# Gated delta stage: triangles of all heads ahead of the state chains, x and half the head tiles through HBM, substitution on 128 partitions, output projection in two halves

## The chip, the cores and the metric

The kernel runs on one core of a Trainium2 chip. The metric is the time of one execution on the device in microseconds; the median of several executions is given, and one execution has been taken with the hardware profiler. Engines: PE (matmuls), DVE, ACT and POOL (elementwise work), SP (issues the DMA transfers). Matmuls write PSUM, everything else is in SBUF, 128 partitions.

## What is computed

A mixer block, an MLP, then a second block with a gated delta rule layer, a feed-forward layer (ffn0), windowed attention, another feed-forward layer and a last norm; 512 positions, width 1024. The change touches the gated delta layer only:

```python
def gated_delta_rule_chunked(q, k, v, beta, g):          # 8 heads of 128, chunks
    gc = jnp.cumsum(g, axis=-1)
    diff = gc[..., :, None] - gc[..., None, :]
    decay = jnp.exp(jnp.where(incl, diff, -jnp.inf))
    kb = k * beta[..., None]
    Lmat = jnp.where(strict, jnp.einsum('bhnid,bhnjd->bhnij', kb, k) * decay, 0.0)
    rhs = jnp.concatenate([v * beta[..., None], kb * jnp.exp(gc)[..., None]], axis=-1)
    sol = lax.linalg.triangular_solve(eye + Lmat, rhs, left_side=True, lower=True, unit_diagonal=True)
    attn_intra = jnp.einsum('bhnid,bhnjd->bhnij', q, k) * decay
    ...
    def step(state, xs):
        v_new = val - jnp.einsum('bhcd,bhde->bhce', kcd, state)
        o = jnp.einsum('bhcd,bhde->bhce', qd, state) + jnp.einsum('bhij,bhje->bhie', a_c, v_new)
        state = state * gl[..., None, None] + jnp.einsum('bhcd,bhce->bhde', kd, v_new)

def deltanet_mixer(h, w_in, conv_w, A_log, dt_bias, onorm_g, w_out):
    p = h @ w_in                        # 8 heads x (k, q, v, gate), and 16 columns for b, a
    qkv = jax.nn.silu(causal_dwconv(qkv, conv_w))        # then l2norm of q and k
    o = gated_delta_rule_chunked(q, k, v, beta, g)
    o = rmsnorm_2(o, onorm_g) * jax.nn.silu(gate)
    return o.reshape(Bsz, S, A_V) @ w_out                # added to x
```

## The kernel before

Activations lie transposed, features on partitions: x is eight tiles `x0` to `x7` of 128 x 512 fp32. A linear layer makes one output tile of 128 x 512 by eight contraction steps of three matmuls of 512 columns each (`mm3`, L266 to L268): both operands are split into a high and a low part, and high by high, low by high and high by low are added in PSUM. Such an output tile, 24 matmuls, is called a unit here. Its weights come by one DMA of 512 KB (L241, on SP's queue); ACT makes the high part (L242) and DVE the low part (L243). Three buffers for weights are in use in turn.

The in projection of the delta layer has 32 such units: k, q, v for each of eight heads (`projected`, after which `conv4` makes the short convolution and its activation), and eight gates (`delta_gate`). Five units (`AHEAD`) are computed in `delta_begin`, then the per-position scalars (`delta_scalars`), and the other 27 are a generator `fill` that serves as filler.

A head goes through four steps. `delta_a` transposes k, q and v by blocks of 128 (L632 is the helper's transposes, L618 that of the outputs), takes squares for the norms, an inverse square root on POOL, builds the decay tile (`decay`), the triangle `LT` and the tile `AT` by small matmuls, writes the diagonal 32 x 32 blocks of `LT` to HBM (L755, four DMAs per head), and scales k and v on ACT (L758, L759) into `kd` and `vb`. `delta_solve(g)` takes the blocks of four heads back, one 32 x 32 triangle per partition on 64 partitions (L773), and inverts them by substitution in 30 steps of two DVE instructions (L780 the outer product, L782 the addition), then sends the result through HBM into the transposed layout (L785, L787). `delta_merge(g)` makes the inverses of 128 x 128 from those of 32 x 32 in small matmuls with copies between (L818, L830, L836, L845, L852). `delta_c(h)` runs the chain over four blocks: state, values, outputs (L868 to L879), each step waiting for a DVE or ACT instruction; at its end come the norm of the output (scaling at L903) and the transposition back. `gated(h)` multiplies by the gate and splits high and low (L300, L301). The output projection (`OutProj` with `a_w_out`, eight units over all heads) adds each unit to x (L967).

`weave` takes generators, each with a count of steps, and interleaves their instructions in proportion to these counts in program order, which is then the order on each engine. The order before: 4 units with `delta_a` of heads 0 and 1; 3 with head 2; 3 with head 3; 6 with the first substitution; 1 with the first merge; 1 with the chains 0 to 3; 3 with heads 4 to 7's triangles; 5 with the second substitution; `gated` 0 to 3; 1 with the second merge; the last ones and four contraction steps of the output projection's first three tiles with the chains 4 to 7; `gated` 4 to 7; the rest of the output projection. SBUF tiles of 128 x 512 come from a pool of 44 (`hid`).

## Time and profile before

| | us |
|---|---|
| median of three executions | 1948.19 (1948.05 to 1948.5) |
| the profiled execution | 1945.63 |
| its span, first to last instruction | 1943.8 |
| PE busy in the span | 1860.1 (96%) |
| DVE busy | 1227.8 (63%) |
| ACT busy | 825.9 (42%) |
| mean granted clock of PE | 0.972 of full speed |

The profile has a page with the busy time of each engine, the span in 40 slices, the DMA queues, the chain of work that ended last, the groups of instructions by line, and the DMA issues. The trace behind it can be asked for stretches, for groups by line and form, for waits and for instructions in order of time. Busy time of PE says that a matmul is under way, not that it runs at full clock: the granted clock stands beside it.

### The profile page before, as it was taken

How to read it: one execution, taken by the hardware profiler on the slowest of the kernel's cores; microseconds unless marked ns; L12 is line 12 of the kernel's file. 1: busy time of each engine (PE TensorE's matmuls, PEld its weight loads, DVE VectorE, ACT ScalarE, POOL GpSimd, SP SyncE). 2: the span in 40 equal slices, each digit the busy share in tenths (PEclk: the TensorE clock that was granted, in tenths of full speed). 3: DMA queues.
4: the chain of work that ended last, by engine and by line, in shares of the span. 5: the costliest groups of instructions: out<-in, count | busy, mean ns of one | idle time of the engine just before them, and what ended most of it. 6: DMA issues, size and time to landing. Idle time of an engine off the chain costs nothing.

```text
span 1943.8 us, 24269 instructions
## 1 busy us (share of the span) xinstructions
PE 1860.1 (96%) x9342; PEld 1559.8 (80%) x9342; DVE 1227.8 (63%) x2259; ACT 825.9 (42%) x1474; POOL 56.9 (3%) x164
## 2 busy tenths in 40 slices
PE   8999999999999989876879999999999999999997
PEld 7887888888889778765767888888888878888887
DVE  7999677324535869567376777743566567777434
ACT  5324453222323775355344444432367544444221
POOL 0010000000000041011000000000000000000000
PEclk9999999999999999789689999999999999999999
DMA  5323322322222222202012223332221123223331
GB/s 173 100 90 98 98 77 97 98 96 91 96 98 85 67 81 94 66 15 74 12 55 88 97 98 98 98 98 97 93 76 35 64 87 98 98 98 98 97 98 55
DMA packets 57427, 166.79 MB, mean 86 GB/s; under 512 B 14560, under 2 KB 17248, under 8 KB 57312
## 3 DMA queue, kind: packets, MB, share of 16 engines
q1 hardware_dynamic: 57312, 165.25, 26.1%
q8 instruction: 73, 1.20, 0.3%
q14 instruction: 42, 0.34, 0.1%
HBM read 162.08 MB, written 3.15 MB: 85 GB/s over the span
## 4 chain that ended last, share of the span: by engine, by line
PE 89%; DVE 5%; ACT 2%; POOL 2%; issue 1%; DMA 1%; DVEq 0%; SPq 0%; ACTq 0%; POOLq 0%
PE m L266 27%; PE m L267 27%; PE m L268 27%; PE a L1193 1%; PE a L1132 1%; PE a L618 1%; PE a L1174 1%; ACT wh L242 1%; DVE outer L780 1%; DVE solve L782 1%; POOL s L325 0%; PE a L873 0%; DVE wl L243 0%; PE a L344 0%; PE a L852 0%
## 5 line engine op out<-in xcount | busy, mean ns | idle before, releaser
L266 PE MATMUL m<-xh,wh 128*128 128x512 f32 (+1 forms) x1560 | 600.4, 388 | 10.4 <-ACT xh L300 6.3
L267 PE MATMUL m<-xl,wh 128*128 128x512 f32 (+1 forms) x1560 | 600.3, 386 | 0.5
L268 PE MATMUL m<-xh,wl 128*128 128x512 f32 (+1 forms) x1560 | 600.2, 386 | 0.2 <-DVE wl L243 0.2
L242 ACT CAST wh<-wr 128x1024 fp32r<-128x1024 f32 x302 | 317.2, 1053 | 618.0 <-PE m L267 492.2
L243 DVE TENSOR_TENSOR wl<-wr,wh 128x1024 fp32r<-128x1024 f32 x302 | 368.4, 1221 | 253.4 <-ACT wh L242 249.6
L267 PE MATMUL m<-h,wh 128*128 128x512 f32 (+1 forms) x984 | 365.0, 371 | 16.5 <-DVE h L301 16.5
L266 PE MATMUL m<-h,wh 128*128 128x512 f32 (+1 forms) x984 | 365.3, 372 | 5.2 <-ACT h L300 3.4
L268 PE MATMUL m<-h,wl 128*128 128x512 f32 (+1 forms) x984 | 364.8, 371 | 0.0
L266 PEld LDWEIGHTS m<-xh,wh 128*128 128x128 f32 x1560 | 293.2, 189 | 70.6 <-ACT xh L300 7.0
L267 PEld LDWEIGHTS m<-xl,wh 128*128 128x128 f32 x1560 | 294.6, 189 | 59.2 <-DVE xl L301 2.3
L268 PEld LDWEIGHTS m<-xh,wl 128*128 128x128 f32 x1560 | 294.5, 189 | 58.9 <-issue 1.0
L267 PEld LDWEIGHTS m<-h,wh 128*128 128x128 f32 x984 | 186.8, 190 | 48.3 <-DVE h L301 16.9
L266 PEld LDWEIGHTS m<-h,wh 128*128 128x128 f32 x984 | 186.5, 190 | 38.8 <-ACT h L300 4.2
L268 PEld LDWEIGHTS m<-h,wl 128*128 128x128 f32 x984 | 186.6, 190 | 32.0 <-DVE wl L243 0.9
L1008 DVE SCALAR_TENSOR_TENSOR t<-t,vecs,t 128x511 f32<-128x511 f32 (+1 forms) x176 | 131.6, 747 | 4.9 <-ACT t L1006 1.8
L1005 DVE TENSOR_TENSOR t<-m,R 128x512 f32<-128x512 f32 x88 | 60.5, 688 | 83.3 <-PE m L268 83.3
L297 ACT CAST h<-t 128x512 fp32r<-128x512 f32 x80 | 49.6, 621 | 145.4 <-DVE t L1016 120.9
L492 DVE SCALAR_TENSOR_TENSOR h<-h,vecs,h 128x511 f32<-128x511 f32 (+28 forms) x120 | 82.3, 728 | 0.9 <-ACT h L489 0.9
L298 DVE TENSOR_TENSOR h<-t,h 128x512 fp32r<-128x512 f32 x80 | 55.1, 689 | 29.7 <-ACT h L297 29.5
L1006 ACT ACTIVATE t<-t,vecs 128x512 f32<-128x512 f32 x88 | 71.6, 814 | 1.8 <-DVE t L1005 1.5
L1014 ACT ACTIVATE t<-t 128x512 f32<-128x512 f32 x44 | 27.8, 632 | 84.9 <-DVE t L1008 84.9
L574 DVE TENSOR_TENSOR t<-m,R 128x512 f32<-128x512 f32 x32 | 22.1, 690 | 58.6 <-PE m L268 56.7
(261 smaller groups left out, 1533.7 us busy)
## 6 DMA issues: line engine op xcount, KB each, us to landing
wr<-in_f_up SPq DMA_DIRECT2D x88, 512.0 KB, 3.5
wr<-in_f_down SPq DMA_DIRECT2D x44, 512.0 KB, 3.5
wr<-in_w_up SPq DMA_DIRECT2D x32, 512.0 KB, 3.5
wr<-in_w_down SPq DMA_DIRECT2D x32, 512.0 KB, 3.4
wr<-in_a_w_in SPq DMA_DIRECT2D x32, 512.0 KB, 3.5
wr<-in_w_in SPq DMA_DIRECT2D x28, 512.0 KB, 3.5
wr<-in_w_o SPq DMA_DIRECT2D x8, 512.0 KB, 3.5
wr<-in_a_w_out SPq DMA_DIRECT2D x8, 512.0 KB, 3.4
```

Of the source, the lines that this page charges most:

```text
L242: nc.scalar.copy(out=wh, in_=raw)
L243: nc.vector.tensor_tensor(out=wl, in0=raw, in1=wh.bitcast(F32), op=ALU.subtract)
L266: nc.tensor.matmul(ps, lhsT=w[0], rhs=x[0], start=start, stop=False)
L267: nc.tensor.matmul(ps, lhsT=w[0], rhs=x[1], start=False, stop=False)
L268: nc.tensor.matmul(ps, lhsT=w[1], rhs=x[0], start=False, stop=stop)
L297: nc.scalar.copy(out=hi, in_=src)
L298: nc.vector.tensor_tensor(out=lo, in0=src, in1=hi.bitcast(F32), op=ALU.subtract)
L492: nc.vector.scalar_tensor_tensor(out=c[:, d:], in0=v[:, :S - d], scalar=wt[CONV_K - 1 - d], in1=c[:, d:], op0=ALU.mult, op1=ALU.add)
L1005: V.tensor_tensor(out=u, in0=ps, in1=R, op=ALU.mult)
L1006: A.activation(out=y, in_=u, func=AF.Identity, scale=w[2], bias=self.vec(f"f_b{i}", c))
L1008: V.scalar_tensor_tensor(out=y[:, d:], in0=u[:, :S - d], scalar=w[2 - d], in1=y[:, d:], op0=ALU.mult, op1=ALU.add)
L1014: A.activation(out=g, in_=g, func=AF.Silu)
```

## The change

- `delta_a` is cut in two. `delta_a` now has the transposes, squares, scalars, the scaling of k and v and the decay tile; `delta_b` has `LT`, `AT` and the DMAs of the diagonal blocks. The scaling is done on POOL, in place, on copies that ACT makes from PSUM.
- Seven units instead of five are made ahead; the scalars are woven with five of them; the two selection tiles are copied on POOL.
- The eight tiles of x come from the pool (now 52), are written to HBM at the start of the stage (`spill`) and read back (`unspill`) after the second substitution; so are `AT` and `kd` of heads 4 to 7.
- `delta_solve` uses 128 partitions: each triangle has its even columns on one partition and its odd ones on another. The same 60 DVE instructions stand in each substitution, over about half the columns; four DMAs instead of one bring the blocks in, two instead of one take them out, and four copies lie around.
- `delta_merge` builds the inverse in `LT`'s own tile. `delta_c` is cut in two: the chain stays, norm and transposition are `delta_d`, and outputs go into q's tile.
- The output projection is two matrices: heads 0 to 3 (`a_w_out0`, eight tiles of 12 matmuls, used as filler H) and heads 4 to 7 (`a_w_out1`, with six accumulators). Each half is added to x.
- The weaves are new: K are k, q and v units, G gates, H tiles of the first half of the output projection.

```diff
-AHEAD = 5
+AHEAD = 7
...
-        self.hp = e(tc.tile_pool(name="hp", bufs=44))
+        self.hp = e(tc.tile_pool(name="hp", bufs=52))
...
-        self.x = [self.cp.tile([P, S], F32, name=f"x{k}") for k in range(NT)]
+        self.x = [self.hid() for _ in range(NT)]
...
+    def spill(self, t):
+        d = self.dp.tile([P, S], F32, tag="spill", name=self.name("spill"), bufs=8)
+        self.nc.sync.dma_start(out=d, in_=t)
+        return d
+
+    def unspill(self, d):
+        t = self.hid()
+        self.nc.sync.dma_start(out=t, in_=d)
+        return t
...
-            A.activation(out=self.blk(kd, b), in_=self.blk(pk, b), func=AF.Copy, scale=rkl[:, b:b + 1])
-            A.activation(out=self.blk(vb, b), in_=self.blk(pv, b), func=AF.Copy, scale=inv[:, b:b + 1])
...
+            nc.gpsimd.tensor_scalar(out=self.blk(kT, b), in0=self.blk(kT, b), scalar1=rkl[:, b:b + 1], scalar2=None,
+                                    op0=ALU.mult)
+            nc.gpsimd.tensor_scalar(out=self.blk(vT, b), in0=self.blk(vT, b), scalar1=inv[:, b:b + 1], scalar2=None,
+                                    op0=ALU.mult)
...
+        if h >= GROUP:
+            s["AT"], s["kd"] = self.spill(E), self.spill(s["kd"])
...
-            w = Q - 1 - j
-            t = self.sized(240, "outer", 2)[0:n, :j * w].rearrange("p (c i) -> p c i", i=w)
-            V.tensor_tensor(out=t, in0=S3[:, j:j + 1, j + 1:].to_broadcast([n, j, w]),
-                            in1=S3[:, 0:j, j:j + 1].to_broadcast([n, j, w]), op=ALU.mult)
-            V.tensor_tensor(out=S3[:, 0:j, j + 1:], in0=S3[:, 0:j, j + 1:], in1=t, op=ALU.add)
+            w, c = Q - 1 - j, (j + 1) // 2
+            row = L[j // h].rearrange("p (j i) -> p j i", i=Q)[:, j % h:j % h + 1, j + 1:]
+            t = self.sized(128, "outer", 2)[:, :c * w].rearrange("p (c i) -> p c i", i=w)
+            V.tensor_tensor(out=t, in0=row.to_broadcast([P, c, w]), in1=W3[:, 0:c, j:j + 1].to_broadcast([P, c, w]),
+                            op=ALU.mult)
+            V.tensor_tensor(out=W3[:, 0:c, j + 1:], in0=W3[:, 0:c, j + 1:], in1=t, op=ALU.add)
...
-        self.weave(units(4), (chain(a(0), a(1)), 2 * SD[0]))
-        self.weave(units(3), (a(2), SD[0]))
-        self.weave(units(3), (a(3), SD[0]))
-        self.weave(units(6), (self.delta_solve(0), 36))
-        self.weave(units(1), (self.delta_merge(0), SD[1]))
-        self.weave(units(1), *((c(h), SD[2]) for h in range(4)))
-        self.weave(units(2), (chain(a(4), a(5)), 2 * SD[0]), (a(6), 2 * SD[0]))
-        self.weave(units(1), (a(7), SD[0]))
-        self.weave(units(5), (self.delta_solve(1), 36))
...
+        w(K(2), A(a(0)))
+        w(K(3), A(a(1), b(0), a(2), b(1)))
+        w(K(1), A(a(3), b(2), b(3)))
+        solve = self.delta_solve(0)
+        w(K(2), (islice(solve, 10), 10))
+        w(K(3), (islice(solve, 14), 14), A(a(4), b(4)))
+        w(K(3), (solve, 10), A(a(5), b(5)))
+        w(K(3), (self.delta_merge(0), SD[1]), A(a(6), b(6)))
+        w(G(1), A(a(7), b(7)))
+        solve = self.delta_solve(1)
+        w(G(2), (islice(solve, 16), 16), C(0), C(1))
+        w(G(2), (solve, 18), C(2), C(3), D(0, 1))
+        w(G(1), D(2, 3), (gated(range(2)), 2))
         for h in range(4, 8):
-            gated(h)
+            for t in ("AT", "kd"):
+                self.heads[h][t] = self.unspill(self.heads[h][t])
+        self.x = [self.unspill(t) for t in self.x]
+        w(G(1), (self.delta_merge(1), SD[1]), (gated(range(2, 4)), 2))
+        out = OutProj(self, self.a["a_w_out1"], os[4:], done)
+        w(join(G(1), H(16)), C(4), C(5))
+        w(H(16), C(6), C(7), D(4, 5))
...
+        out.grow(3)
+        w((out.head(2), 12), D(6, 7))
...
         out.rest()
```

The lines of the kernel shift: `mm3` is at L272 to L274 after, the merge's matmuls at L865, L884, L893 and L900, the substitution's instructions at L819 and L821, the chains' matmuls from L916 on, the decay's at L720 and L721.

PE before, from the end of the first merge (L845, L852) to the first steps of the chains (L873, L878); `a` is a PSUM tile for small products, `h` an SBUF tile, `x4` stands for four alike:

```order
L845 MATMUL a_6570<-solve_6424,h_5444 64x64 x4
L845 MATMUL a_6570<-solve_6424,h_5613 64x64 x4
L852 MATMUL a_6581<-h_6428,h_6571 64x64 x4
L852 MATMUL a_6581<-h_6430,h_6571 64x64 x4
L845 MATMUL a_6595<-solve_6424,h_5816 64x64 x4
L845 MATMUL a_6595<-solve_6424,h_6025 64x64 x4
L852 MATMUL a_6609<-h_6432,h_6596 64x64 x4
L852 MATMUL a_6609<-h_6434,h_6596 64x64 x4
L873 MATMUL a_6633<-h_5459,h_6428 128x128
L873 MATMUL a_6637<-h_5628,h_6430 128x128
L873 MATMUL a_6641<-h_5831,h_6432 128x128
L878 MATMUL a_6633<-h_5459,h_5458 128x128
```

PE after, at the same steps of the first merge (L845 and L852 are L893 and L900 there); `m` is the PSUM tile of a unit:

```order
L272 MATMUL m_6938<-xh_4802,wh_6940 128x512
L273 MATMUL m_6938<-xl_4803,wh_6940 128x512
L274 MATMUL m_6938<-xh_4802,wl_6941 128x512
L272 MATMUL m_6938<-xh_4804,wh_6940 128x512
L273 MATMUL m_6938<-xl_4805,wh_6940 128x512
L274 MATMUL m_6938<-xh_4804,wl_6941 128x512
L893 MATMUL a_6954<-h_6659,h_5961 64x64 x4
L893 MATMUL a_6954<-h_6659,h_5990 64x64 x4
L638 MATMUL a_6966<-h_6454 128x128 x4
L272 MATMUL m_6938<-xh_4806,wh_6940 128x512
L273 MATMUL m_6938<-xl_4807,wh_6940 128x512
L274 MATMUL m_6938<-xh_4806,wl_6941 128x512
```

Units and the transposes and decay tile of head 6 now stand between the merge's steps, where before one step of merge or chain followed the other.

DVE before, in the second substitution, heads 4 to 7 (`solve` is the tile of triangles, `outer` the product):

```order
L780 TENSOR_TENSOR outer1305_7630<-solve1263_7448 64x168
L782 TENSOR_TENSOR solve1263_7448<-solve1263_7448,outer1305_7630 64x24x7
L780 TENSOR_TENSOR outer1306_7636<-solve1263_7448 64x150
L782 TENSOR_TENSOR solve1263_7448<-solve1263_7448,outer1306_7636 64x25x6
L780 TENSOR_TENSOR outer1307_7642<-solve1263_7448 64x130
L782 TENSOR_TENSOR solve1263_7448<-solve1263_7448,outer1307_7642 64x26x5
L780 TENSOR_TENSOR outer1308_7651<-solve1263_7448 64x108
L782 TENSOR_TENSOR solve1263_7448<-solve1263_7448,outer1308_7651 64x27x4
L780 TENSOR_TENSOR outer1311_7661<-solve1263_7448 64x84
L784 MEMSET solve1263_7448 64x32
L782 TENSOR_TENSOR solve1263_7448<-solve1263_7448,outer1311_7661 64x28x3
```

DVE after, there:

```order
L819 TENSOR_TENSOR outer1279_7489<-h1221_7167,h1222_7168 128x84
L950 TENSOR_TENSOR s1290_7525<-s1289_7524 128x4
L930 SCALAR_TENSOR_TENSOR h998_5889<-h998_5889,d875_5253,a1281_7496 128x128
L821 TENSOR_TENSOR h1222_7168<-h1222_7168,outer1279_7489 128x12x7
L951 TENSOR_TENSOR s1290_7525<-s1290_7525,s1288_7523 128x4
L938 SCALAR_TENSOR_TENSOR h923_5470<-a1280_7492,d873_5251,h923_5470 128x128
L819 TENSOR_TENSOR outer1282_7500<-h1221_7167,h1222_7168 128x78
```

Between the two instructions of a step now stand the updates of the chains 2 and 3 (L930, L938) and the norms of heads 0 and 1 (L950, L951); the product of the same step (168 elements before, 84 after) is half as wide.

SP before, from the second substitution's result to the weights that follow:

```order
L241 DMA wr1434_8416<-in_a_w_out 128x1024
L785 DMA scr873_5285<-solve1263_7448 64x1024
L787 DMA h1318_7688<-scr873_5285 128x16x32
L241 DMA wr1438_8448<-in_a_w_out 128x1024
L241 DMA wr1442_8480<-in_a_w_out 128x1024
L241 DMA wr1477_8603<-in_f_up0 128x1024
```

SP after, there (`h` at L655 are the tiles read back):

```order
L247 DMA wr1394_8170<-in_a_w_out0 128x1024
L829 DMA scr891_5351<-h1220_7166 64x512
L829 DMA scr891_5351<-h1221_7167 64x512
L832 DMA h1300_7602<-scr891_5351 128x16x32
L247 DMA wr1412_8283<-in_a_w_out0 128x1024
L655 DMA h1328_7745<-spill1088_6378 128x512
L655 DMA h1329_7747<-spill1089_6380 128x512
```

Fourteen more reads like the last two follow (the other tiles of heads 4 to 7, then x), and only then the weights `a_w_out1` of the second half of the output projection; those of the first half are ahead of them.

## Rows read from the trace of the kernel before

**Rows 1.** Page, part 1: busy time, share, instructions of each engine.

```profile
PE 1860.1 (96%) x9342; PEld 1559.8 (80%) x9342; DVE 1227.8 (63%) x2259; ACT 825.9 (42%) x1474; POOL 56.9 (3%) x164
```

**Rows 2.** By stretches: us, busy (count) of each engine, clock, DMA share, GB/s.

```profile
653.30:741.00 87.70, 80.69 (x406) 66.94 (x406) 65.03 (x133) 72.15 (x179) 26.65 (x68) 0.98 0.23 71
741.00:793.50 52.50, 52.50 (x233) 43.47 (x232) 49.23 (x103) 19.29 (x26) 0.00 (x0) 1.00 0.29 97
793.50:818.50 25.00, 16.93 (x232) 15.84 (x230) 6.10 (x17) 9.02 (x21) 2.37 (x5) 0.58 0.25 65
818.50:842.00 23.50, 19.16 (x141) 17.94 (x140) 14.90 (x70) 13.95 (x63) 0.00 (x0) 0.94 0.00 1
842.00:910.50 68.50, 59.88 (x300) 48.86 (x300) 40.18 (x128) 45.17 (x144) 15.84 (x68) 0.93 0.17 48
910.50:934.50 24.00, 3.87 (x9) 2.35 (x9) 19.02 (x51) 2.69 (x6) 2.38 (x5) 0.57 0.24 64
934.50:953.70 19.20, 19.20 (x233) 17.09 (x233) 4.09 (x15) 7.11 (x18) 0.00 (x0) 0.50 0.00 1
953.70:976.00 22.30, 22.30 (x157) 21.33 (x156) 10.24 (x37) 9.79 (x37) 0.00 (x0) 0.90 0.01 2
976.00:991.00 15.00, 4.53 (x18) 2.79 (x16) 12.89 (x81) 6.46 (x32) 0.00 (x0) 0.58 0.00 0
991.00:1043.90 52.90, 51.09 (x215) 40.71 (x216) 33.84 (x55) 23.07 (x34) 0.00 (x0) 0.96 0.28 90
sum 390.60, PE 330.15 PEld 277.32 DVE 255.54 ACT 208.69 POOL 47.23; mean PE 25.40 PEld 21.33 DVE 19.66 ACT 16.05 POOL 3.63
```

**Rows 3.** PE in order of time (start, duration), from small matmuls to big ones.

```profile
673.70 1.05 PE L632 MATMUL a<-h 128*128 128x128 f32 x8
674.50 0.47 PE L266 MATMUL m<-xh,wh 128*128 128x512 f32 x1
674.82 0.39 PE L267 MATMUL m<-xl,wh 128*128 128x512 f32 x1
```

**Rows 4.** Chain of waits, 786 to 846 us: start, duration, what ran.

```profile
793.40 4.24 DMA scr<-solve
797.65 3.31 DMA h<-scr
```

**Rows 5.** Waits of PE, 793 to 1031 us: us, times, longest.

```profile
PE m L267 <- DVE h L301: 16.5, 1, 16.5
PE a L618 <- DVE h L903: 15.5, 6, 3.6
```

**Rows 6.** DVE by line and form, 653 to 1044: busy, mean ns, idle.

```profile
L780 DVE TENSOR_TENSOR outer<-solve 64x240 f32<-64x240 f32 x4 | 1.6, 398 | 0.1
L780 DVE TENSOR_TENSOR outer<-solve 64x30 f32<-64x30 f32 x4 | 0.8, 192 | 0.2
```

**Rows 7.** The same view of DVE: weights' low part, adds to x.

```profile
L243 DVE TENSOR_TENSOR wl<-wr,wh 128x1024 fp32r<-128x1024 f32 x38 | 46.3, 1220 | 7.7 <-ACT wh L242 7.4
L967 DVE TENSOR_TENSOR x<-m,x 128x512 f32<-128x512 f32 x8 | 5.5, 690 | 13.1 <-PE m L268 13.1
```

**Rows 8.** The same view of ACT: the scaling of k.

```profile
L758 ACT ACTIVATE h<-a,hs 128x128 f32<-128x128 f32 x32 | 12.2, 381 | 13.6 <-POOL hs L743 13.5
```

**Rows 9.** The same view of POOL, 640 to 1050 us.

```profile
L326 POOL TENSOR_SCALAR s<-s 128x8 f32<-128x8 f32 x24 | 6.8, 285 | 1.9
L811 POOL MEMSET h<- 128x512 f32 x8 | 3.8, 515 | 0.0
```

**Rows 10.** SP in order of time; the page's DMA issues, us to landing.

```profile
739.85 1.75 SPq L755 DMA_DIRECT2D scr<-h  x4
...
wr<-in_a_w_in SPq DMA_DIRECT2D x32, 512.0 KB, 3.5
```

**Rows 11.** DVE by line and form, 1100 to 1200, POOL idle.

```profile
L243 DVE TENSOR_TENSOR wl<-wr,wh 128x1024 fp32r<-128x1024 f32 x19 | 23.3, 1225 | 2.2 <-ACT wh L242 1.7
```

More of the change, by code (lines that the diff above doesn't have):

```diff
@@ L830, in delta_merge @@
             T.matmul(p[0:Q, i * Q:(i + 1) * Q], lhsT=TTq[q[1], i], rhs=Mq[q[1], i], start=True, stop=True)
[L831 removed]
+        for k, t in enumerate(T64):
+            A.copy(out=t[q[1], :, 0:Q], in_=half(cq(p)[0:Q], k))
         yield
@@ L980, in delta, with unit @@
-        self.weave(units(1), (a(7), SD[0]))
-        self.weave(units(5), (self.delta_solve(1), 36))
-        for h in range(4):
-            gated(h)
-        self.weave(units(1), (self.delta_merge(1), SD[1]))
-        def rest():
-            yield from fill
-            yield from out.head(4)
-        self.weave((rest(), NT + 12), *((c(h), SD[2]) for h in range(4, 8)))
-        for h in range(4, 8):
-            gated(h)
+        def unit(u):
+            if u < 3 * HEADS:
+                return self.lin_steps(st, u, xs, lambda ps: self.projected(u, ps, R))
+            return self.delta_gate(st, [u - 3 * HEADS], xs, R)
@@ new lines, in first @@
+        def first():
+            so = self.stream(self.a["a_w_out0"], NT // 2)
+            for m in range(NT):
+                yield from self.lin_steps(so, m, os[:4], lambda ps, m=m: done(m, ps))
+        kqv = iter(range(AHEAD, 3 * HEADS))
+        gate = iter(range(3 * HEADS, 4 * HEADS))
+        half = first()
+        K = lambda n: (chain(*(unit(next(kqv)) for _ in range(n))), n * NT)
+        G = lambda n: (chain(*(unit(next(gate)) for _ in range(n))), n * NT)
+        H = lambda n: (islice(half, n), n)
@@ new lines, in delta @@
+        join = lambda *jobs: (chain(*(j[0] for j in jobs)), sum(j[1] for j in jobs))
+        a, b, c = self.delta_a, self.delta_b, self.delta_c
+        w = self.weave
+        self.x = [self.spill(t) for t in self.x]
+        C = lambda h: (c(h), 11)
+        D = lambda *hs: (chain(*(self.delta_d(h) for h in hs)), 2 * len(hs))
+        A = lambda *jobs: (chain(*jobs), sum(5 if j.__name__ == "delta_a" else 2 for j in jobs))
+        w(K(2), A(a(0)))
+        w(K(3), A(a(1), b(0), a(2), b(1)))
@@ new lines, in delta @@
+        for h in range(4, 8):
+            for t in ("AT", "kd"):
[5 more added lines that the diff above has]
+        w(H(16), C(6), C(7), D(4, 5))
+        for _ in gated(range(4, 6)):
+            pass
+        out.xs = os[4:]
+        out.grow(3)
@@ L993, in delta @@
+        w((out.head(2), 12), D(6, 7))
+        for _ in gated(range(6, 8)):
+            pass
+        out.xs = os[4:]
         out.rest()
```

151 lines of the change are left out of this document (96 added, 55 removed).

## Prediction

> **What bounds the kernel now.** I read the page's busy shares first: PE is busy 1860.1 of 1943.8 us, DVE 63%, ACT 42%, POOL 3% [rows 1]. A kernel that is 96% matmul can gain only where PE idles, or where it runs at less than its full clock. So the second view is the table by stretches of the only part in which both happen, the gated delta rule with its in and out projections, from 653.3 us (the weave of in-projection units with the triangles) to 1043.9 us (the first units of the next feed-forward block) [rows 2]. In each line the reader should multiply PE's busy time by the granted clock: that is the matmul work in microseconds of full clock (2.4 GHz is 1.00, 1.2 GHz is 0.50). Down the column: 79.1, 52.5, 9.8, 18.0, 55.7, 2.2, 9.6, 20.1, 2.6, 49.0, together 298.6. The part takes 390.6, so 92.0 are lost: 60.4 idle (390.6 less the sum of 330.15) and 31.6 at a low clock. The loss of each stretch is its length less that product: 8.6, 0, 15.2, 5.5, 12.8, 21.8, 9.6, 2.2, 12.4, 3.9.
>
> Four places hold 59 of the 92. The return of the first substitution and its merge (793.5 to 818.5, 15.2 lost): the chain of waits shows the result going out in 4.24 and coming back in 3.31 us, with nothing else for PE [rows 4], and the merge that follows runs at a mean clock of 0.58. The end of the second substitution (910.5 to 934.5, 21.8 lost): PE has 9 matmuls in 24 us, and the waits give one idle time of 16.5 us for the low half of a gated head, a DVE instruction that stands behind the substitution in DVE's order [rows 5]. The second merge (934.5 to 953.7): PE never idles and works all 19.2 us at 1.2 GHz, after the idle 24 us; 9.6 lost. The norms and gates of heads 4 to 7 (976 to 991, 12.4 lost): PE waits for DVE's scaling of the outputs, 15.5 us in six waits over the whole part [rows 5]. What is lost is thus a matter of order: PE's big matmuls are used up elsewhere when these stages come.
>
> **The change, part by part.** *Order.* No matmul is added or removed: 27 units of 24 matmuls before, 25 behind seven instead of five ahead, and the output projection keeps its 192. They are moved, so that units stand between the steps of both merges, beside the second substitution and between the chains' steps. What this costs PE: in the part, PE goes from big matmuls to small ones or back 243 times, where it did 109 times. After a row of eight transposes of 128x128 (0.80 us in all), the first big matmul takes 0.32 us to the start of the next [rows 3], against 52.50/233 = 0.225 in the dense stretch [rows 2]: 0.09 for a return. For a departure I take 0.03 (0 and 0.09 are the ends). 134 more switches, half of each kind, 0.06 each: 8 us (6 to 12). Work: 306.6.
>
> *Substitution on 128 partitions.* 60 steps of two DVE instructions stay. 64x240 takes 398 ns and 64x30 takes 192 (means of one) [rows 6]: about 1 ns an element of a partition and 0.16 fixed. The mean width falls from 157 to 87 elements, so 120 instructions go from 38 to 30 us. The length of the dependent chain falls by 4 us for each half of the heads. The four more DMAs and the copies around them add about 2 us to the way out and back for each, which was 7.5 [rows 4].
>
> *Extra adds.* Since the first half of the heads is added to x on its own, DVE has 16 adds in place of 8, at 690 ns [rows 7]: +5.5 us, half of them under output matmuls, the last 8 where the old 8 were. *Selection tiles* go from DVE to POOL: about -2. DVE thus stays near 255 us of 350, and is nowhere the bound of the whole; it is close in the stretch with chains 0 to 3, the second substitution and norms 0 to 3: 15 for the substitution, some 12 for chains (14.90 in the whole stretch 818.5 to 842 [rows 2]), 5 for four low weight halves at 1220 ns [rows 7], some 7 for norms and gates, 39 in all, against about 21.6 (96 matmuls at 0.225) and 13.5 (19.16 busy times 0.94 [rows 2], less a unit's 5.4, rounded up for the switches), 35, of PE.
>
> *Scaling to POOL.* ACT loses 64 scalings of 381 ns [rows 8], 24 us, and gains 16 copies of 128x512, each at most four times such a scaling: 24 us at the most, so no more work than before. POOL gains 64 of 128x128. No such instruction of POOL is in the trace; 285 ns for 128x8 and 515 for a memset of 128x512 [rows 9] bound it to 0.29 and 0.52; I take 0.4, near ACT's 381 ns for the same shape: 26 us. Nothing waits for them soon (the keys go to the spill, or to chains a unit or more later), so I price them at 0; uncovered they would stand ahead of the chains at 8 times 0.4, 3 us a head.
>
> *Spilling.* 16 tiles of 256 KB go out and 16 come back. SP takes 0.44 us for an issue (1.75 for four), and 512 KB land in 3.5 us [rows 10]: 7 us of issuing and 28 of transfer for the reloads. They stand on SP behind the second substitution's result; the weights of the output projection's first half are all issued ahead of them, and the second half's behind them, needed only after two units, the merge and 96 output matmuls. The first reload with a near user is x's first tile, ninth in the row, some 16 us after its issue, needed when the first output unit ends, some 20 us after. So 0; if it landed with the last of the 16, after 28 us, PE would lose 8, since DVE would stand at the add with the chains' updates queued behind it.
>
> **The losses after**, against the old ones. Front, with scalars and triangles 0 to 3: 8 (8.6 before; the same kind of weave). First substitution with triangles 4 and 5: 5 (0 before, but DVE now has about 55 us beside 57 of PE). Merge 0 with two triangles: 4 of the old 15.2; three to nine big matmuls, 0.7 to 2 us, now stand over each step's copy. Chains 0 to 3, second substitution, norms: 7 of 27.3, mostly DVE's 39 over 35. Merge 1: 5, since one unit has to cover it, with gated heads behind each other on DVE. Chains 4 to 7 beside the first half of the output projection: 4. The last norms: 5 of 12.4 (a chain of some 13 us over 36 matmuls, 8 us). Start of the feed-forward block: 5, as 3.9 before plus adds. Low clock: 4 of 31.6, since PE is not left idle ahead of the merges. Together 47. The part would take 306.6 + 47 = 353.6, a gain of 37.0. The profiled execution (1945.63) would become 1908.6, the median of the runs, 2.6 above it, **1911**.
>
> **Rivals.** *Denser.* The stretch from 741 to 793.5 loses nothing at all beside a substitution [rows 2]. If the weaves after do as well, and only the front, the last norms and the block's start lose, 20 in place of 47: a gain of 64, 1884. Against it speaks that no stretch with triangles in it was clean.
>
> *The weave drags.* Of the old stretches the one most like the new ones is 842 to 910.5, with triangles 4 to 7 and a substitution: 12.8 lost on 55.7 of work, 23%. At that rate 306.6 would lose 70.5, a gain of 13.5, 1935; with the reloads late, 1943, still faster, by about the bound below.
>
> *POOL in DVE's way.* In the old trace DVE's subtraction with two inputs takes 1220 ns in this part, where POOL is busy 47 us [rows 2, 7], and 1225 where POOL is idle [rows 11]: no sign of it. But POOL never worked on 128x128 there. If POOL's 26 us held up DVE one for one and half of that were on PE's path, 13 of gain would go: 1924. The Trainium skill has this as a rule: "SBUF — State Buffer", section "SBUF: two separate sides", says that VectorE and Pool share a pair of ports under an exclusive lock, so that a VectorE instruction with two SBUF inputs and a Pool instruction that reads SBUF block each other for their whole length. By that rule the time is this rival's, 1924 or more; the trace of before does not bear it out, its 1220 against 1225 ns.
>
> *Slower, by the clock.* The second merge shows that PE busy all of 19.2 us can run at 1.2 GHz after an idle stretch [rows 2]. Small dependent matmuls now are scattered over the whole part. If PE were left at 1.2 GHz from the first merge to the end of the output projection, each microsecond of work there costs one more. With no low clock at all the part would gain 37 + 4 = 41, so this decides from 41 us of work done at 1.2 GHz. Half of the work that the merges, chains and output stretches hold now (9.8, 18.0, 2.2, 9.6, 20.1, 2.6 and 49.0, 111 in all) is 56, which gives 1948 + 15 = 1963. Against it: the mixed stretches 842 to 910.5 and 653.3 to 741 had 0.93 and 0.98.
>
> *That the change does not do what it says:* the order of the instructions has the units between the merges' steps, so this is left at nothing.
>
> **How the numbers follow.** My own case 0.62 (1895 to 1925, from 31 to 61 of losses), denser 0.10, dragging 0.14, POOL 0.06, clock 0.08. A measurement of this kernel can tell about 0.2%, 4 us. Faster: my case, denser, POOL, and 0.11 of dragging, 0.89; same: dragging with the reloads late, 0.03; slower: the clock, 0.08. The range goes from the denser case with the switches at their 6, 1882, to the dragging one, 1936. It leaves out the clock's 0.08 and some 0.05 each of the densest and the most dragging.
>
> **What would show it.** Right: in the table by stretches, PE's work over the part near 307, idle near 43, the granted clock above 0.95 in both merges, no wait of PE over 5 us behind the second substitution; the substitution's instructions at a mean near 250 ns; DVE's 1220 ns unchanged beside a busy POOL; x's add not waiting for a reload. Wrong: a clock of 0.5 in a merge, PE waiting for the key copies (POOL), or DVE busy over 90% in the middle stretches with PE idle by as much.

## The result and the profile after

The changed kernel takes 1877.49 us (median; 1874.66 to 1877.67), the kernel before 1948.12 beside it on the same chip. The ratio is 0.9634, with a 95% interval of 0.9618 to 0.9651: some 71 us less, where 37 were forecast. The time lies 5 us below the range. The direction and the place were right, the size was not. Both profiled executions lie some 3 us below the medians (1945.63 and 1874.66 us).

The first line is part 1 of the page of the changed kernel, which answers [rows 1]:

```profile
PE 1842.2 (98%) x9342; PEld 1542.8 (82%) x9342; DVE 1220.2 (65%) x2275; ACT 817.5 (44%) x1439; POOL 94.0 (5%) x226
```

PE is busy 18 us less with the same number of matmuls, and its share rises to 98%. The table by stretches answers [rows 2]. Stretches were laid at the same places of the program: front with scalars and triangles 0 to 3; first substitution; first merge with triangle 6; the rest of those units with triangle 7; chains 0 to 3 with the second substitution; its norms and the way back; second merge; chains 4 to 7; last norms and end of the output projection; start of the feed-forward block.

```profile
653.44:729.50 76.06, 74.61 (x389) 62.49 (x389) 59.97 (x123) 58.95 (x148) 40.00 (x97) 1.00 0.25 76
729.50:785.00 55.50, 52.70 (x254) 43.69 (x252) 50.29 (x133) 37.37 (x87) 24.53 (x56) 0.97 0.39 116
785.00:803.50 18.50, 18.41 (x223) 15.19 (x223) 7.60 (x19) 11.11 (x36) 7.89 (x25) 0.72 0.11 33
803.50:824.60 21.10, 21.04 (x138) 17.58 (x139) 12.06 (x28) 14.35 (x38) 4.96 (x20) 1.00 0.24 78
824.60:866.70 42.10, 41.61 (x249) 35.45 (x248) 37.10 (x159) 21.85 (x70) 4.01 (x7) 1.00 0.25 78
866.70:885.00 18.30, 17.70 (x82) 13.97 (x80) 15.20 (x57) 10.84 (x27) 0.66 (x2) 1.00 0.90 288
885.00:901.00 16.00, 16.00 (x235) 13.61 (x234) 4.83 (x11) 6.67 (x16) 0.00 (x0) 0.69 0.26 99
901.00:935.20 34.20, 34.20 (x212) 30.26 (x213) 24.61 (x88) 17.75 (x60) 0.00 (x0) 0.95 0.14 47
935.20:960.50 25.30, 23.96 (x107) 18.88 (x106) 21.23 (x60) 15.42 (x33) 0.00 (x0) 1.00 0.25 77
960.50:973.60 13.10, 13.09 (x62) 10.93 (x63) 11.66 (x21) 5.73 (x8) 0.00 (x0) 1.00 0.27 94
sum 320.16, PE 313.33 PEld 262.04 DVE 244.55 ACT 200.06 POOL 82.06; mean PE 31.33 PEld 26.20 DVE 24.46 ACT 20.01 POOL 8.21
```

The part took 390.6 us and takes 320.2: 70.4 of the 70.9 by which the span shrank (1943.8 to 1872.9). Read as before, busy time times clock gives 299.9 of work (298.6 before). What is lost is 20.2: 6.8 idle (60.4 before) and 13.4 at a low clock (31.6 before). The forecast had 43 idle and 4 by the clock.

The waits of PE in the part have all but gone. These are the largest of the changed kernel, from 653 to 975 us (who waits, for whom; us in all, times, longest), against 16.5 and 15.5 in [rows 5]:

```profile
PE a L624 <- ACT h L615: 2.8, 1, 2.8
PE m L272 <- DVE h L985: 1.2, 1, 1.2
PE m L272 <- DVE h L1036: 1.1, 1, 1.1
```

| stretch | lost before | forecast | lost after |
|---|---|---|---|
| front, triangles 0 to 3 | 8.6 | 8 | 1.5 |
| first substitution, triangles | 0 (and 12.8 with triangles 4 to 7) | 5 | 4.4 |
| return and first merge | 15.2 | 4 | 5.3 |
| chains 0 to 3, second substitution, norms | 5.5 + 21.8 | 7 | 1.1 |
| second merge | 9.6 | 5 | 5.0 |
| chains 4 to 7 | 2.2 | 4 | 1.7 |
| last norms | 12.4 | 5 | 1.3 |
| start of the feed-forward block | 3.9 | 5 | 0 |
| low clock, over the whole | in the rows | 4 | in the rows |

The losses before and after hold what the low clock costs; the forecast set its stretches against such losses and put 4 for the clock beside them.

### The profile page after: what moved, and what is told of

Its sections match the earlier page's. It is cut to its first block, busy times and chain, and to the rows that moved or that the text cites. A ratio compares the mean times of both kernels' runs of the same rounds, so it can differ in the third digit from the quotient of the medians.

```text
span 1872.9 us, 24384 instructions
## 1 busy us (share of the span) xinstructions
PE 1842.2 (98%) x9342; PEld 1542.8 (82%) x9342; DVE 1220.2 (65%) x2275; ACT 817.5 (44%) x1439; POOL 94.0 (5%) x226
## 4 chain that ended last, share of the span: by engine, by line
PE 89%; DVE 7%; ACT 2%; issue 1%; POOL 1%; DMA 0%; DVEq 0%; ACTq 0%
PE m L272 27%; PE m L273 27%; PE m L274 27%; PE a L1290 1%; DVE t L613 1%; DVE wl L249 1%; PE a L1229 1%; PE a L1271 1%; PE a L624 1%; ACT wh L248 1%; PE a L350 0%; PE a L921 0%; PE a L927 0%; PE a L919 0%; PE a L916 0%
## 5 line engine op out<-in xcount | busy, mean ns | idle before, releaser
L272 PE MATMUL m<-xh,wh 128*128 128x512 f32 (+1 forms) x1560 | 603.5, 390 | 10.3 <-ACT xh L306 6.0
L274 PE MATMUL m<-xh,wl 128*128 128x512 f32 (+1 forms) x1560 | 600.3, 386 | 0.2 <-DVE wl L249 0.2
L249 DVE TENSOR_TENSOR wl<-wr,wh 128x1024 fp32r<-128x1024 f32 x302 | 368.7, 1222 | 247.3 <-ACT wh L248 243.8
L272 PE MATMUL m<-h,wh 128*128 128x512 f32 (+1 forms) x972 | 361.0, 372 | 1.8 <-DVE h L1128 0.9
L274 PE MATMUL m<-h,wl 128*128 128x512 f32 (+1 forms) x972 | 359.7, 370 | 0.0
L273 PE MATMUL m<-h,wh 128*128 128x512 f32 (+1 forms) x972 | 359.6, 370 | 0.0
L272 PEld LDWEIGHTS m<-xh,wh 128*128 128x128 f32 x1560 | 292.9, 189 | 69.9 <-ACT xh L306 8.9
L274 PEld LDWEIGHTS m<-xh,wl 128*128 128x128 f32 x1560 | 294.5, 189 | 57.8 <-issue 0.7
L272 PEld LDWEIGHTS m<-h,wh 128*128 128x128 f32 x972 | 183.8, 189 | 33.1 <-issue 2.0
L274 PEld LDWEIGHTS m<-h,wl 128*128 128x128 f32 x972 | 183.8, 189 | 30.6 <-DVE wl L249 0.5
L273 PEld LDWEIGHTS m<-h,wh 128*128 128x128 f32 x972 | 184.0, 189 | 30.2 <-issue 0.7
L1102 DVE TENSOR_TENSOR t<-m,R 128x512 f32<-128x512 f32 x88 | 60.4, 688 | 80.0 <-PE m L274 78.2
```

The source lines that it names most:

```text
L249: nc.vector.tensor_tensor(out=wl, in0=raw, in1=wh.bitcast(F32), op=ALU.subtract)
L272: nc.tensor.matmul(ps, lhsT=w[0], rhs=x[0], start=start, stop=False)
L273: nc.tensor.matmul(ps, lhsT=w[0], rhs=x[1], start=False, stop=False)
L274: nc.tensor.matmul(ps, lhsT=w[1], rhs=x[0], start=False, stop=stop)
L1102: V.tensor_tensor(out=u, in0=ps, in1=R, op=ALU.mult)
```

## The experiments

Each run is given by its ratio to the kernel before, with its interval; the changed kernel has 0.9634 (0.9618 to 0.9651). One thousandth is 1.9 us. Differences under some 3 us are not resolved. In two runs (the first merge without units, the first half of the output projection behind the chains) the interval overlaps that of the changed kernel; there all four executions still lie above its four.

### Scaling of k and v back on ACT

```diff
-            nc.gpsimd.tensor_scalar(out=self.blk(kT, b), in0=self.blk(kT, b), scalar1=rkl[:, b:b + 1], scalar2=None,
-                                    op0=ALU.mult)
...
+            A.activation(out=self.blk(kT, b), in_=self.blk(kT, b), func=AF.Copy, scale=rkl[:, b:b + 1])
+            A.activation(out=self.blk(vT, b), in_=self.blk(vT, b), func=AF.Copy, scale=inv[:, b:b + 1])
```

> The changed kernel with the 64 scalings of k and v back on ACT, in place on the copies; POOL keeps only the small scalars. ACT gets some 24 us more work, three quarters of it in the first 76 us of the stage, where it is busy 59. Cover theory: 0 to 2 us slower, 1877 to 1880. Rival: relieving ACT is a part of the gain, 10 us or more slower, 1887 or more. Second rival, POOL in DVE's way: without POOL's 49 us DVE gets faster and the time falls by 2 us or more, with the two-input subtraction of the weights under 1215 ns.

0.971 (0.9695 to 0.9724), 1890.27 us: 13 to 15 us slower. In this run the waits of ACT from 653 to 840 us show why; then a wait of DVE in the same stretch:

```profile
ACT h L763 <- POOL hs L760: 14.6, 7, 3.3
...
ACT h L764 <- POOL hs L760: 2.1, 1, 2.1
...
DVE t L613 <- ACT t L611: 23.4, 10, 7.0
```

ACT stands 16.7 us at the scalings for POOL's chain of small scalars. Behind them in ACT's order are the convolutions' first steps (L611), for which DVE then waits 23.4 us (7.6 in the changed kernel). The first instruction of the substitution starts at 751.8 us, in the changed kernel at 738.5: 13.3 of the 14.5 us between the two profiles are there. My expectation for cover, 0 to 2 us, was wrong, and the rival's "10 or more" right; but its reason, the amount of work, was still to be told from the wait. The second rival did not show: DVE's subtraction has a median of 1222 ns without POOL's scalings and 1219 with them.

The second form takes the copies out too and scales straight from PSUM, as the kernel before did:

```diff
-        A.copy(out=kT, in_=pk)
...
-        A.copy(out=vT, in_=self.transpose4(s["v"]))
+        pv = self.transpose4(s["v"])
...
+            A.activation(out=self.blk(kT, b), in_=self.blk(pk, b), func=AF.Copy, scale=rkl[:, b:b + 1])
+            A.activation(out=self.blk(vT, b), in_=self.blk(pv, b), func=AF.Copy, scale=inv[:, b:b + 1])
```

> The changed kernel with k and v scaled on ACT straight from PSUM, as the kernel before did: no 16 copies, no scaling on POOL. Theory now (from the trace of e2_scale_act): the scalings wait for POOL's chain of small scalars, and on ACT all that is queued behind them waits too (weights' high halves, squares, convolutions), 13 us in that run; then this run, which keeps that wait, is 9 to 15 us slower than the changed kernel, 1886 to 1892. Rival: it is ACT's amount of work; without the copies (10 us less than e2_scale_act) it is at most 5 us slower, 1882 or less.

0.9737 (0.9722 to 0.9751), 1895.42 us: 18 to 20 us slower, beyond both bounds. ACT has 10 us less work than in the first form and the kernel is slower, so it is not the amount. Waits of ACT (653 to 840), then of PE (653 to 985):

```profile
ACT h L762 <- POOL hs L759: 13.4, 4, 4.1
ACT h L763 <- POOL hs L759: 12.2, 3, 5.6
...
PE a L624 <- ACT h L762: 7.0, 2, 4.0
```

ACT now stands 25.6 us for POOL, and PE's next transposes wait for these scalings, since they hold the PSUM tile. The first substitution starts at 751.8 us here too; the second ends 6 us later than in the first form. The row had been before my eyes: 13.5 us of ACT's idle time ahead of L758 were put down to POOL [rows 8].

### POOL's scaling, and the cut triangles, alone in the kernel before

The first of two: the same copies and POOL scaling, put into the kernel before, nothing else.

> The kernel before with one part of the change alone: k and v are copied from PSUM by ACT at once and scaled in place on POOL. ACT's wait for POOL's scalars there was 13.5 us. If this wait is worth its length on PE's path, 10 to 14 us faster than before, 1934 to 1938. If PE waits there mostly for the triangle product on DVE, which still waits for POOL, 2 to 6 us faster, 1942 to 1946.

1.0021 (1.0012 to 1.0031): 4 us slower, outside both expectations. The second adds the cut of `delta_a` in two, each triangle one head behind its scalars:

```diff
-        self.weave(units(4), (chain(a(0), a(1)), 2 * SD[0]))
-        self.weave(units(3), (a(2), SD[0]))
-        self.weave(units(3), (a(3), SD[0]))
+        self.weave(units(4), (chain(a(0), a(1), b(0)), 10))
+        self.weave(units(3), (chain(a(2), b(1)), 6))
+        self.weave(units(3), (chain(a(3), b(2), b(3)), 8))
...
+        self.weave(units(2), (chain(a(4), a(5), b(4), a(6), b(5)), 16))
+        self.weave(units(1), (chain(a(7), b(6), b(7)), 8))
```

> The kernel before with scaling on POOL (as f1_before_pool) and the triangles cut in two, each head's product one head behind its scalars; all else as before. Theory: what PE lost in the weaves with triangles (8.6 and 12.8 us before) was DVE standing at the triangle product for POOL's scalars (21 us); with the distance POOL's queue has room, and 6 to 14 us go: 1933 to 1941. Rival: the cost seen in f1_before_pool stays, 1945 to 1951.

0.9963 (0.9949 to 0.9977), 1940.49 us: 7 us faster than before and 10 to 11 faster than the first. One row each tells most of both, PE's wait for the triangle product on DVE (653 to 1045), in the kernel before, with POOL's scaling, and with the cut as well:

```profile
PE a L618 <- DVE h L751: 6.4, 4, 2.7
```

```profile
PE a L618 <- DVE h L757: 11.5, 3, 5.3
...
DVE h L757 <- POOL hs L746: 20.8, 5, 5.8
```

```profile
PE a L618 <- DVE h L763: 2.1, 1, 2.1
```

Eight scalings of some 0.6 us a head stand in POOL's queue ahead of the next head's scalars, where heads follow closely; the triangle product on DVE waits for those, and PE's transposes for that product. With the product one head later PE hardly waits for it, though DVE still waits 16.6 us for POOL; the wait for the gated head [rows 5] also falls, from 16.2 in the first run to 12.6, and one of 5.4 for weights' low halves is new. POOL's scaling is thus worth something there only with the cut; the cut alone was not run.

### The distance of the triangles, and the front, undone in the changed kernel

```diff
-        w(K(2), A(a(0)))
-        w(K(3), A(a(1), b(0), a(2), b(1)))
-        w(K(1), A(a(3), b(2), b(3)))
+        w(K(2), A(a(0), b(0)))
+        w(K(3), A(a(1), b(1), a(2), b(2)))
+        w(K(1), A(a(3), b(3)))
```

> The changed kernel with each head's triangle (b) right behind its scalars (a) for heads 0 to 3, instead of one head later. In the kernel before DVE's triangle product waited 21 us for POOL's scalars, and PE's transposes 6.4 us for that product. If the distance between a and b is what removed this, the wait of DVE for POOL goes from 3 to over 10 us and the time up by 4 to 8 us, 1881 to 1886. Rival: the scheduler finds other work meanwhile, 0 to 2 us: 1877 to 1880.

0.9638 (0.9623 to 0.9652): no difference. DVE's wait for POOL rises from 3.3 to 6.7 us only, and PE waits for the triangle product nowhere. The distance within a head does not matter for heads 0 to 3 here. That they stand further apart is not the reason: their products start 11 to 15 us apart in this run, 15 to 19 in the kernel before. Which edit took PE's wait away at the front is thus not shown; not tried alone is the place of the decay tile, which now stands behind the scalars and stood ahead of them.

```diff
-AHEAD = 7
+AHEAD = 5
...
-        self.weave((more(), NT * (AHEAD - 2)), (scalars(), 5))
+        for _ in chain(more(), scalars()):
+            pass
...
-        w(K(2), A(a(0)))
+        w(K(4), A(a(0)))
```

> The changed kernel with five units ahead instead of seven, the per-position scalars in a row behind them instead of woven, and the two units beside head 0's triangles. Cover theory: the front's loss goes back from 1.5 to about 8 us (8.6 before), 1883 to 1886. Rival: the cut of the triangles in two did it and the scalars' place does not matter: 1877 to 1879.

0.9638 (0.9623 to 0.9652): no difference either. The place of the scalars and the two units ahead gave nothing that can be measured.

### The substitution on 64 partitions

The old `delta_solve`, in the changed kernel.

> The changed kernel with the substitution back on 64 partitions (60 DVE instructions over twice the columns, about 4.4 us more DVE work for each half of the heads; one DMA in, one out). Cover theory: what the change won is that big matmuls stand beside every serial chain, and DVE has slack there (37.1 busy of 42.1 us beside chains 0 to 3); so 0 to 3 us slower, 1877 to 1881. Rival: the shorter substitution is itself a large part of the gain, since it was the chain that PE waited for; then at least 9 us slower, 1886 or more.

0.9641 (0.9626 to 0.9655): no difference. DVE is busy 36.95 of 42.1 us in the stretch with the chains 0 to 3, 37.10 in the changed kernel: the room was there.

### The first merge without units

```diff
-        w(K(3), (self.delta_merge(0), SD[1]), A(a(6), b(6)))
+        w((self.delta_merge(0), SD[1]))
+        w(K(3), A(a(6), b(6)))
```

> The changed kernel with the first merge written ahead of its three units instead of woven with them. In the order on PE 43 big matmuls stand ahead of the merge's first, as before (39), and the merge's matmuls follow each other with two groups of four big ones between, where there were five groups of 3 to 16. If units between the merge's steps are what the change won there, as the prediction said, the loss goes from 5 us back toward 15: 1885 to 1888. If only the return of the result had to be covered, 0 to 3 us: 1877 to 1881, with the clock in the merge lower than 0.72.

0.9663 (0.9646 to 0.9679), 1880.75 us: 3 to 6 us slower, between the two expectations. The stretch with the merge in this run:

```profile
785.00:812.00 27.00, 26.77 (x278) 23.23 (x277) 10.46 (x22) 11.59 (x37) 0.98 (x2) 0.68 0.12 40
```

PE is busy nearly all of it at a clock of 0.68; the profile of the changed kernel has 0.72 over 18.5 us. That difference need not be the edit's. Within the first merge, the stretch at 1.2 GHz lasts 10.3 us in that profile, but 17.1 in this run and just as long in the run with the triangles joined, whose first merge is woven as in the changed kernel. The changed kernel, that run and this one:

```profile
788.60:798.90 10.30, 10.30 (x100) 8.40 (x96) 3.40 (x10) 5.23 (x19) 4.14 (x19) 0.50 0.13 45
...
787.90:805.00 17.10, 17.06 (x137) 13.70 (x137) 4.04 (x10) 8.34 (x30) 7.90 (x25) 0.50 0.09 32
...
790.80:807.90 17.10, 17.10 (x137) 14.80 (x135) 3.21 (x9) 4.89 (x20) 0.00 (x0) 0.50 0.05 19
```

What only this run has there is a wait of PE of 3.0 us behind the merge, for a head's convolution on ACT:

```profile
PE a L624 <- ACT h L615: 3.0, 1, 3.0
```

The return of the result needs no units between the merge's steps, since those of the units that are ready go ahead of it on PE. That units between the steps save clock is not shown.

### The chains 0 to 3 back behind the first merge

```diff
-        w(G(1), A(a(7), b(7)))
-        solve = self.delta_solve(1)
-        w(G(2), (islice(solve, 16), 16), C(0), C(1))
-        w(G(2), (solve, 18), C(2), C(3), D(0, 1))
-        w(G(1), D(2, 3), (gated(range(2)), 2))
+        w(G(1), C(0), C(1), C(2), C(3))
+        w(G(1), A(a(7), b(7)))
+        solve = self.delta_solve(1)
+        w(G(4), (solve, 34), D(0, 1, 2, 3))
+        for _ in gated(range(2)):
+            pass
```

> The changed kernel with the chains 0 to 3 where they stood before: together behind the first merge, beside one unit, ahead of head 7's triangles; the second substitution then has four gate units and the norms 0 to 3 beside it, but no chains. Cover theory: the four chains lose their old 5 us again, with a clock below 0.95, and the second substitution, 60 instructions in a row with 22 us of big matmuls beside it, some 2 to 6: 1884 to 1889. Rival: the place of the chains gave nothing, 0 to 2 us.

0.9706 (0.9692 to 0.9721), 1889.79 us: 12 to 14 us slower, at the upper end of what cover foretold. Four stretches of this run, the end of the chains, head 7's triangle, the second substitution, the second merge:

```profile
815.00:840.00 25.00, 24.97 (x185) 23.18 (x185) 15.86 (x46) 13.06 (x50) 0.00 (x0) 1.00 0.20 65
840.00:860.00 20.00, 17.32 (x85) 13.94 (x84) 12.36 (x55) 12.08 (x35) 8.85 (x25) 1.00 0.37 109
860.00:890.00 30.00, 24.55 (x109) 18.95 (x108) 27.93 (x120) 12.53 (x31) 0.60 (x2) 0.94 0.27 94
890.00:915.00 25.00, 23.13 (x250) 19.49 (x249) 7.43 (x20) 9.84 (x25) 0.00 (x0) 0.64 0.55 183
```

Beside the substitution DVE is busy 27.93 of 30 us and PE idles 5.5. Nearly all of this is one wait at the substitution's end, for the high half of a gated head, much as in the kernel before [rows 5]:

```profile
PE m L272 <- ACT h L306: 4.9, 1, 4.9
```

The edit also takes the gated heads 0 and 1 out of their weave, so the place of the chains and that of these heads are not told apart. The stretch with the second merge behind it has a clock of 0.64. The chains themselves lost next to nothing (24.97 of 25.00 us busy at a clock of 1.00): the expectation's total was about right, its first term wrong.

### The output projection: first half behind the chains, and three accumulators

```diff
-        w(join(G(1), H(16)), C(4), C(5))
-        w(H(16), C(6), C(7), D(4, 5))
+        w(G(1), C(4), C(5), C(6), C(7))
+        w(H(32))
+        w(D(4, 5))
```

> The changed kernel with the first half of the output projection behind the chains 4 to 7 instead of beside them; the four chains run together beside one unit, as chains 0 to 3 did before. Cover theory: the old losses of such chains come back, 5.5 of the four chains alone, and a lower clock in them, 5 to 9 us: 1882 to 1887. Rival: the scheduler brings other matmuls ahead anyway, 0 to 2 us: 1877 to 1880.

0.966 (0.9646 to 0.9675), 1880.14 us: 3 to 5 us slower, below most of what cover foretold and above the rival. Too near to the bound to say more.

```diff
-        out.grow(3)
-        w((out.head(2), 12), D(6, 7))
+        out.grow()
+        w((out.head(2), 6), D(6, 7))
```

> The changed kernel with three accumulators instead of six for the second half of the output projection, so that half as many matmuls of it (18 instead of 36) are ready beside the last norms. Cover theory: 4 us of cover less, 3 to 5 us slower, 1880 to 1883. Rival: the last norms are short enough by now, 0 to 2 us.

0.9665 (0.9651 to 0.968), 1882.52 us: 5 to 6 us slower, as cover foretold. From the last norms to the start of the feed-forward block PE idles 3.4 us in this run (32.80 less 29.39), with the clock at 0.95; the changed kernel idles 1.3 there at full clock:

```profile
935.20:968.00 32.80, 29.39 (x132) 23.58 (x131) 27.22 (x71) 19.32 (x40) 0.00 (x0) 0.95 0.21 72
```

### The reload twice

```diff
-        self.nc.sync.dma_start(out=t, in_=d)
+        for _ in range(2):
+            self.nc.sync.dma_start(out=t, in_=d)
```

> The changed kernel with each of the 16 reads back from HBM done twice, 4.2 MB and some 28 us of transfer more on the queue ahead of the weights of the output projection's second half. If the spilling is off the path with room to spare, 0 to 2 us slower, 1877 to 1880. If it is only just covered (the prediction had 16 us of transfer under some 20 of other work for x's first tile), PE waits for an addition to x or for those weights, 8 us or more slower, 1885 or more.

0.9639 (0.9624 to 0.9653): no difference. In a stretch from the end of the second substitution into the merge, here in this run and then in the changed kernel, PE idles 0.6 us in both:

```profile
866.70:901.00 34.30, 33.69 (x310) 27.86 (x310) 22.06 (x75) 18.75 (x48) 0.84 (x2) 0.90 0.78 235
...
866.70:901.00 34.30, 33.70 (x315) 27.58 (x314) 20.03 (x68) 17.52 (x42) 0.66 (x2) 0.85 0.60 200
```

The rest of the added traffic comes later: SP issues the 32 reads from 875.4 to 904.9 us, and the weights behind them at 905.0.

### What a change between big and small matmuls costs

Idle transposes are added to the last feed-forward layer, where PE is the bound: one behind each contraction step, or eight behind each unit.

```diff
+        extra = lambda k: self.nc.tensor.transpose(self.blk(d, k % 4), self.ident, self.ident)
         for k in range(NT):
             self.mm3(ps, st(m, k), xs[k], k == 0, k == NT - 1)
+            extra(k)
```

> The changed kernel with 352 idle transposes of 128x128 added to the up projection of the last feed-forward layer, one behind each contraction step's three matmuls of 512 columns (704 changes between big and small). To be compared with s2_bunched. With the prediction's price of 0.06 us for a change, 352 x (0.10 + 0.12) = 77 us over the changed kernel; if a change is free beside the small matmul's own 0.10 us, 35 us.

> The same 352 transposes, eight in a row behind each of the 44 units (88 changes). With the prediction's price 352 x 0.10 + 44 x 0.12 = 40 us over the changed kernel, 37 us below s1_scattered; if a change is free, 35 us, and the same as s1_scattered.

Scattered 1924.55 us (0.9886; 0.9871 to 0.9901), bunched 1917.52 (0.9851; 0.9834 to 0.9867): 47 and 40 us over the changed kernel. The price of 0.06 had 77 and 40, a free change 35 for both, so the scattered run refutes the price and the bunched one alone would not. The same work differs by 7.0 us for 616 changes: 0.011 us each, if all cost the same. In a row of eight, a transpose starts some 0.11 us behind the one before (1.04 us less the last one's 0.27, by seven), not 0.10; then the 352 of them are 39 us by themselves, which leaves 8 us for the 704 changes and 1 for the 88, some 0.01 each. PE in order of time (start, duration), scattered and then bunched:

```profile
1700.07 0.40 PE L274 MATMUL m<-xh,wl 128*128 128x512 f32 x1
1700.31 0.27 PE L293 MATMUL a<-c 128*128 128x128 f32 x1
1700.34 0.48 PE L272 MATMUL m<-xh,wh 128*128 128x512 f32 x1
1700.65 0.39 PE L273 MATMUL m<-xl,wh 128*128 128x512 f32 x1
```

```profile
1703.10 1.04 PE L293 MATMUL a<-c 128*128 128x128 f32 x8
1703.89 0.47 PE L272 MATMUL m<-xh,wh 128*128 128x512 f32 x1
1704.20 0.39 PE L273 MATMUL m<-xl,wh 128*128 128x512 f32 x1
```

The big matmul does take 0.31 us to the next start. But it starts 0.03 us after the single small one, whose own 0.11 us are thus seen in the next interval: small and big together take 0.34, which is what 0.11 and 0.23 add up to.

## Why the prediction was wrong

**What held.** The place (all but 0.5 us of the gain lies in the part from 653 us), the waits that would go (rows 2, 4 and 5), the price of 0 for the spilling, and the small part of the substitution on 128 partitions: 64 partitions and a doubled reload change nothing. (The mean width before is 165 elements, not 157; its 120 instructions take 38.6 and 29.6 us in the traces, where 38 and 30 were forecast.) The merges' total came out too (9 forecast, 10.3 measured with the return), but by accident, as shown below.

**The losses after: 47 forecast, 20.2 measured. This step failed.** With the changes between big and small matmuls (8 forecast, 1.3 measured) it makes up all of the miss, 37.0 for 70.4. Of the 26.8 us too much, 6.5 are at the front, 5.9 at the chains 0 to 3 with the second substitution, 5 at the start of the feed-forward block, 3.7 at the last norms, 2.3 at the chains 4 to 7, and 4 are the row for the low clock, which the measured losses hold already; the first substitution and the merges together were put 0.7 too low.

The step priced woven stretches by what woven stretches had lost before (8 for the front "the same kind of weave", 5 or 7 for others, the dragging rival at 23%). That carried over a loss without asking whose it was. At the front PE idled 7.0 us in the kernel before (87.70 less 80.69 [rows 2]), and most of it was a wait for the triangle product on DVE, which waited for POOL's chain of scalars (653 to 741 us):

```profile
PE a L618 <- DVE h L751: 5.5, 3, 2.7
...
DVE h L751 <- POOL hs L744: 8.3, 3, 3.4
```

With the triangles of heads 4 to 7 such waits of PE were 3.7 of 8.6 us idle, so there this chain was less than half. Over the whole part it held up DVE for 21.3 us at the triangle product, and ACT for 13.5 us at the scalings [rows 8]:

```profile
DVE h L751 <- POOL hs L744: 21.3, 7, 4.5
```

The change takes the wait out of ACT's order and puts distance into DVE's. The prediction priced the move of the scalings at nothing, "Nothing waits for them soon", and gave the cut of the triangles no price. It asked who would wait for the moved instructions, and not who had been queued behind them where they stood. Put back on ACT they cost 13 to 15 us, straight from PSUM 18 to 20. In the kernel before POOL's scaling without the distance loses 4 us, with it the two gain 7; in the changed kernel the distance of heads 0 to 3 can go without loss.

**DVE's 39 us over PE's 35** in the middle stretch did not bind: 41.6 us of PE over 37.1 of DVE, 1.1 us lost for 7 forecast. The run with the chains put back, where less work of PE stands beside the substitution, cost 12 to 14.

**The last norms, and the start of the next block:** 1.3 for 5 and 0 for 5. The 36 matmuls beside the norms, which I had set at 8 us against a chain of 13, were enough; with half of them the kernel takes 5 to 6 us more. No run undoes what took the loss from the next block's start.

**Low clock: 4 forecast, 13.4 measured.** Its reason, "since PE is not left idle ahead of the merges", fell. The second merge follows a stretch with 17.70 of 18.30 us busy at 1.00, is itself busy 16.00 of 16.00, and has 0.69; the first has 0.72 with 18.41 of 18.50 busy. These means hold both levels of the clock. The second merge:

```profile
885.00:891.00 6.00, 6.00 (x173) 5.65 (x172) 2.27 (x5) 3.49 (x10) 0.00 (x0) 1.00 0.69 262
891.00:901.00 10.00, 10.00 (x66) 7.96 (x64) 2.56 (x6) 3.18 (x7) 0.00 (x0) 0.50 0.00 1
```

The clock stays at 1.2 GHz up to 904.7 us. So the prediction's own sign of being wrong, a clock of 0.5 in a merge, did show. The merges' total came out right by accident: their loss was put down to idle time between steps, and it is clock. The order on PE shows what stands there: the units that are ready go ahead while the result is on its way back, and in the second merge 176 products of 32 x 32 or 64 x 64 blocks then follow each other without a big matmul between (885.3 to 891.7 us); it is among these that the clock falls. In the profiles of two runs that take the changed kernel's time the first merge spends some 7 us more at 1.2 GHz than here, so that 13.4 can be 3 us more in other executions.

**The changes between big and small: 8 forecast, 1.3 more work measured** (no more than the rounding of the clock in the rows), and 0.011 us each in the two runs, 1.5 for 134. The start-to-start interval behind a small matmul was read as a cost, and it holds that matmul's own work.

**POOL's scaling** takes 0.75 to 0.79 us where I took 0.4 and bounded it by 0.52, so this bound was wrong too; PE did not wait for it, and DVE 3.3 us in all. Of the rivals, "denser" (1884) had the right total of losses (20) by luck: it left them to the front, the last norms and the block's start, which lose 2.8 together, while the merges lose 10.3. What separates its time from the measured one is the 6.7 us of changes that do not exist.

What stays open: the single edits undone cost 18 to 20, 12 to 14, 5 to 6, and 3 to 6 twice, together 41 to 51 us of the 71, if they add. The rest (the return of the first result with nothing beside it, the start of the next block, and most of the wait for the gated heads behind the substitution) was not undone by any run; that it went is shown by the rows, what each was worth alone is not.

## What to carry to other kernels

A loss in a woven stretch belongs to a wait: before it is carried over to another order, look up whose wait it was, and whether the change removes it. When an instruction moves to another engine, price what was queued behind it on the old one, above all if it stood there waiting for a third engine. An edit can be worth something only together with another, and where matmuls differ in size their cost is read from a group from first start to the next group's start, not from one interval.

## What the runs showed of the hardware

POOL's 128 x 128 scaling takes 0.60 us at the median, but up to 2.3 when DVE works beside it. POOL, then DVE in the changed kernel (start, duration):

```profile
691.44 2.31 POOL L763 TENSOR_SCALAR h<-h,hs 128x128 f32<-128x128 f32 x2
693.73 0.60 POOL L765 TENSOR_SCALAR h<-h,hs 128x128 f32<-128x128 f32 x1
```

```profile
691.29 1.22 DVE L249 TENSOR_TENSOR wl<-wr,wh 128x1024 fp32r<-128x1024 f32 x1
692.42 0.86 DVE L613 SCALAR_TENSOR_TENSOR t<-t,vecs,t 128x509 f32<-128x509 f32 x1
```

Spans on POOL are rough in the profile. Two scalings last 2.31 us while DVE has two instructions with two SBUF inputs; the next ones take 0.60. The Trainium skill ("SBUF — State Buffer", section "SBUF: two separate sides") says that the two engines lock each other out of a shared pair of ports; the trace agrees for POOL, which pays; for DVE it shows little of it. The second of the two DVE instructions takes 0.86 us, where the median of its line is 0.75, and DVE's subtraction keeps its time: a median of 1219 ns from 685 to 830 us with the scalings on POOL, 1222 with them on ACT.

PE's clock was granted at 0.69 of full speed on average in a merge that PE spent busy from end to end, without an idle stretch ahead of it: full for the first 6 us, then 1.2 GHz. In the kernel before the same merge had 0.50, after 24 us with nine matmuls [rows 2].
